# An encoder layer in one core: the down projection as seven half-depth products for eight, with its weights' sums kept in DRAM

## The chip, the cores and the metric

The kernel runs on one core of one Trainium2 chip. Its time is the device time of one execution in microseconds; before the change it is 1742.5 us, the median of three runs (1742.41 to 1742.98).

The engines of the core: TensorE (PE; PEld is its weight load) multiplies matrices into PSUM, which has eight banks of 2 KB per partition; VectorE (DVE), ScalarE (ACT) and GpSimd (POOL) work elementwise; SyncE (SP) issues DMAs, as ACT and GpSimd may too. Each engine takes its own instructions strictly in order, and a waiting instruction holds everything behind it.

## The reference

One layer on two sequences of 1024 and 256 tokens, T = 1280 in all, in float32: a wide input projection, neighbourhood attention and a gated short convolution, their merge, an output projection and a LayerNorm, and then the part that the change touches:

```python
h = dwconv3(x @ ffn_w_up + ffn_b_up, ffn_conv_w, ffn_conv_b)      # 1024 -> 2 x 2816
h_gate, h_val = jnp.split(h, 2, axis=-1)
f = (jax.nn.gelu(h_gate) * h_val) @ ffn_w_down + ffn_b_down       # 2816 -> 1024
return layer_norm(DEEPNORM_ALPHA * x + f, ln2_g, ln2_b)
```

The gated h is 2816 wide, that is 22 k-tiles of 128; w_down is 2816 x 1024; the result has ten token tiles of 128 x 1024.

## The kernel before

Every matmul of float32 data is made in three passes of a shorter float type: an operand is split into a high part (ACT's cast) and a low part (DVE's subtraction), `split2`, and high x high, low x high and high x low are added in PSUM (`passes`, L57). The order of all engines is written out by hand (`tc.manual_schedule`): the order in which the Python code issues an instruction is the order on its engine. Tiles come from pools with a fixed number of buffers; an instruction that writes a buffer waits until the last user of the old contents is done.

The stages in order: V and the first splits (to 60 us); the input projection, 18 pairs of column tiles (60 to 503 us); attention, with the convolution branch's product beside it (to 830 us); the merge, the output projection, the first LayerNorm (to 900 us); the up projection, 22 pairs (to 1428 us); the down projection and the second LayerNorm (to the end).

Both wide projections already use a seven-product scheme (class `Sevens`): weights and activations are cut in quarters, sums of quarters are formed, and seven products of half size stand for eight. A product is a slot of 24 matmuls of 320 columns; `at_slot(n, f)` puts side work behind slot n's weights and evictions. In slot n, ACT and DVE prepare the weights of product n+2 (`weights`) and evict product n-1 (`evict`, L154). The input projection has 126 slots; the pairs of gates are in slots 70 to 125. V is written to `v_dram` by `v_out` and read back in parts of four head pairs (`v_load`, `v_split`); the first part is loaded in slot 112 (NS - 14) into a pool of its own (vfp).

The up projection ends in a convolution, a gelu on ACT, a product on GpSimd, and a store of each of the 22 tiles of h to `h_dram` (L958 to L960). The down projection (L1012 to L1242) is a plain product. It takes the ten token tiles in three groups of 4, 3 and 3; a group holds two PSUM banks for each tile (two halves of 512 columns) and runs over the 22 k-tiles:

```python
for n in range(n0, n0 + FFT - DEEP):
    for at, t in enumerate(ts):
        for half in range(2):
            dn_mm(banks[t, half], n, at, half, n == n0, False)
    dn_next()
```

`dn_next` loads and splits a k-tile of h and of w_down a few steps ahead (`dn_split`: `fh`/`fl`, `wd`); the first ten w_down tiles stay in SBUF for the later groups, the others are loaded and split again. The last five k-tiles of a group are taken token by token, and after each token comes the second LayerNorm (`token`): sum (L1147), `mean` (ACT squares and centres, GpSimd multiplies by the gain, L1158), `var` and `rstd`, `finish` on DVE for 768 columns (L1161) and `finish_pool` on GpSimd for the rest (L1165), and the store. DVE has one list for all of this: splits, residual sums, evictions and LayerNorm stand one behind another.

Of the kernel before, what the change touches and what calls it, by code (L numbers as in the profile page):

```python
# [39 lines left out]
def encoder_kernel(ctx: ExitStack, tc: tile.TileContext, a: dict, y_prompt, y_sample):  # L40
# [352 lines left out]
    def yc_load(j):  # L393
        ycf.append(up_tile("o"))
        nc.sync.dma_start(out=ycf[j], in_=yc_dram[j])
# [68 lines left out]

    C0, REST = slice(0, 512), slice(512, T)
    for n, f in ((NS - 14, lambda: v_load(0)), (NS - 6, lambda: (yc_load(0), yc_load(1))), (NS - 5, lambda: (yc_load(2), yc_load(3)))):
        pr7.at_slot(n, f)
# [46 lines left out]
    for j in range(2, NP):  # L514
        yc_split(j, REST)
    up.release()
# [10 lines left out]
    at.tile([P, NT, P], F32, tag="vf", name="vf")  # L527
# [139 lines left out]
    v_split(0, 0)  # L667
    head_load(1)
    for n in range(units + LAG_V):
# [4 lines left out]
        if n == 1:  # L674
            v_split(0, 1)
# [29 lines left out]
    vfp.release()  # L705
# [306 lines left out]
    GROUPS = (range(0, 4), range(4, 7), range(7, NT))  # L1012
    DEEP = 5
    RES, NRING, NH = 10, 6, DEEP + 3
    ND = len(GROUPS) * FFT
    hs, ws, loaded = {}, {}, {}

    def dn_load(n):
        if n >= ND:
            return  # L1020
        g, i = divmod(n, FFT)
        c0, cn = GROUPS[g][0] * P, len(GROUPS[g]) * P
        hr = dnraw[:, 2, n % 2 * 512:n % 2 * 512 + cn]
        nc.sync.dma_start(out=hr, in_=h_dram[i][:, c0:c0 + cn])
        wr = None
        if g == 0 or i >= RES:
            wr = dnraw[:, n % 2, :]
            nc.sync.dma_start(out=wr, in_=a["w_down"][i * P:(i + 1) * P, :])
        loaded[n] = hr, wr, cn

    def dn_split(n):
        if n >= ND:
            return
        i = n % FFT
        hr, wr, cn = loaded.pop(n)
# [35 lines left out]
    for n in range(NS + 3):  # L1071
# [21 lines left out]
        if n == NS - 5:  # L1093
            for m in range(2):
                dn_load(m)
        if n == NS - 3:
# [6 lines left out]
            dwb = pool("dwb")  # L1103
        run_slot(n)
        if NS - 3 <= n <= NS:
# [8 lines left out]
    ss, zs, ys = [], [], {}  # L1114
# [4 lines left out]
    def residual_rows(n):  # L1119

        if n == 1:
            bd.append(dy.tile([P, D], F32, tag="z", name="bd", bufs=3))
# [5 lines left out]
        if n == 11:  # L1128
# [228 lines left out]
```

## Time and profile before

| | |
|---|---|
| profiled execution | 1741.4 us, span 1739.6 us |
| median of three runs | 1742.5 us |
| TensorE busy | 1693.5 us (97%), 10080 matmuls |
| DVE, ACT, GpSimd busy | 67%, 39%, 26% |
| DMA | 203.5 MB, mean 117 GB/s |

A busy matmul is counted from its start to a modelled end, and the matmuls overlap; what one costs is the spacing of starts. Shares of a stage are read from the table by stretches, not from the page's totals. In that table "PEclk" is the granted TensorE clock (1.00 is 2.4 GHz), "DMA share" the mean busy share of 16 DMA engines.

### The profile page before, as it was taken

To read this page: it belongs to the slowest core of one execution; us is meant where nothing else is said; L and a number is where in the kernel's file an instruction comes from. 1 tells how busy PE (TensorE), PEld (TensorE's weight loads), DVE (VectorE), ACT (ScalarE), POOL (GpSimd) and SP (SyncE) were. 2 spreads that over 40 slices of the span, in tenths; PEclk is the share of its full clock that TensorE was granted. 3 is DMA by queue.
4 is the path that set the end of the run, shared out by engine and by line. 5 is a ranking of instruction groups with operands and counts; after the bars stand their busy time and mean duration, and the time that the engine had idled before them with its cause. 6 is when DMAs were issued, how large, how long until landed. Compare 5 with 4: busy or idle time off the path is not lost.

```text
span 1739.6 us, 25955 instructions
## 1 busy us (share of the span) xinstructions
PE 1693.5 (97%) x10080; PEld 1567.2 (90%) x10080; DVE 1168.3 (67%) x1828; ACT 671.2 (39%) x1068; POOL 454.3 (26%) x368
## 2 busy tenths in 40 slices
PE   9999999999999998999998999999999999999997
PEld 7999999999988886778798999999999998888886
DVE  8466567434467774754698888888888887545455
ACT  4423323333246774323453333333333344333332
POOL 1222122212226663500113323332333220030202
PEclk9999999999999997999999999999999999999999
DMA  6276121222285632332301212211222137516262
GB/s 221 85 230 196 58 80 49 99 97 105 74 319 182 197 108 92 137 135 82 136 14 66 69 63 67 79 68 59 72 79 68 52 121 234 212 57 224 89 213 89
DMA packets 68923, 203.53 MB, mean 117 GB/s; under 512 B 7360, under 2 KB 19904, under 8 KB 68800
## 3 DMA queue, kind: packets, MB, share of 16 engines
q1 hardware_dynamic: 63040, 177.75, 30.3%
q0 software_dynamic: 3456, 15.73, 2.6%
q10 hardware_dynamic: 2304, 8.39, 1.2%
q8 instruction: 80, 1.31, 0.3%
q14 instruction: 43, 0.35, 0.1%
HBM read 145.48 MB, written 56.36 MB: 116 GB/s over the span
## 4 chain that ended last, share of the span: by engine, by line
PE 86%; DVE 7%; issue 3%; ACT 3%; DMA 1%; POOL 0%; ACTq 0%; POOLq 0%; DVEq 0%; SPq 0%
PE ps_x L57 52%; PE ps_dn L57 17%; PE ps_o L57 3%; PE ps_v L57 3%; PE ps_ch L548 3%; PE ps_ch L57 2%; PE o_ps L57 2%; PE s_ps L57 1%; PE t_ps L605 1%; DVE ul L69 1%; DVE c L154 1%; DVE xl L69 1%; DVE ml L69 0%; PE pz L844 0%; DMA x_dram<-ya 0%
## 5 line engine op out<-in xcount | busy, mean ns | idle before, releaser
L57 PE MATMUL ps_x<-xh,ul 128*128 128x320 f32 x2240 | 695.1, 310 | 8.0 <-DVE ul L69 7.5
L57 PE MATMUL ps_x<-xh,uh 128*128 128x320 f32 x2240 | 693.0, 309 | 3.7 <-ACT uh L72 3.1
L57 PE MATMUL ps_x<-xl,uh 128*128 128x320 f32 x2240 | 693.1, 309 | 1.9 <-DVE xl L69 1.9
L57 PEld LDWEIGHTS ps_x<-xh,ul 128*128 128x128 f32 x2240 | 421.9, 188 | 13.7 <-DVE ul L69 13.7
L57 PEld LDWEIGHTS ps_x<-xh,uh 128*128 128x128 f32 x2240 | 421.9, 188 | 4.5 <-ACT uh L72 3.7
L57 PEld LDWEIGHTS ps_x<-xl,uh 128*128 128x128 f32 x2240 | 421.8, 188 | 3.0 <-DVE xl L69 3.0
L69 DVE TENSOR_TENSOR ul<-ur,uh 128x512 fp32r<-128x512 f32 x240 | 199.4, 832 | 207.3 <-ACT uh L72 207.0
L72 ACT CAST uh<-ur 128x512 fp32r<-128x512 f32 x240 | 147.5, 616 | 330.1 <-PE ps_x L57 287.4
L57 PE MATMUL ps_dn<-wd,fh 128*128 128x512 f32 x880 | 271.4, 389 | 1.3 <-DVE dnraw L154 1.3
L154 DVE TENSOR_TENSOR c<-ps_x,c 128x640 f32<-128x640 f32 x275 | 220.6, 813 | 0.4 <-PE ps_x L57 0.3
L57 PEld LDWEIGHTS ps_dn<-wd,fh 128*128 128x128 f32 x880 | 165.2, 188 | 36.3 <-issue 1.0
L129 POOL TENSOR_TENSOR ur<-ur 128x512 f32<-128x512 f32 x40 | 56.5, 1414 | 510.1 <-DVE ul L69 510.1
L57 PE MATMUL ps_dn<-wd,fl 128*128 128x512 f32 x440 | 171.2, 389 | 0.0
L69 DVE TENSOR_TENSOR ul<-us,uh 128x512 fp32r<-128x512 f32 x38 | 71.0, 1867 | 55.1 <-ACT uh L72 55.1
L57 PEld LDWEIGHTS ps_dn<-wd,fl 128*128 128x128 f32 x440 | 82.6, 188 | 17.0
L943 ACT ACTIVATE o<-c,vec 128x1280 f32<-128x1280 f32 x43 | 62.5, 1458 | 83.8 <-DVE c L154 83.8
L946 DVE SCALAR_TENSOR_TENSOR o<-c,vec,o 128x1023 f32<-128x1023 f32 x86 | 89.2, 1037 | 1.6 <-ACT o L943 1.6
L959 POOL TENSOR_TENSOR o<-o 128x1280 f32<-128x1280 f32 x22 | 65.4, 2974 | 93.5 <-ACT o L958 80.8
L1158 POOL TENSOR_TENSOR z<-z,g 128x1024 f32<-128x1024 f32 (+1 forms) x10 | 23.2, 2316 | 252.9 <-issue 158.8
L1048 DVE TENSOR_TENSOR wd<-dnraw,wd 128x1024 fp32r<-128x1024 f32 x46 | 56.1, 1220 | 36.6 <-ACT wd L1047 36.5
L947 DVE SCALAR_TENSOR_TENSOR o<-c,vec,o 128x1023 f32<-128x1023 f32 x86 | 77.9, 905 | 3.0
L592 POOL TENSOR_TENSOR sp<-sp,stat 128x384 f32<-128x384 f32 (+1 forms) x80 | 59.5, 746 | 72.5 <-DVE stat L591 52.3
(202 smaller groups left out, 2341.9 us busy)
## 6 DMA issues: line engine op xcount, KB each, us to landing
dnraw<-in_w_down SPq DMA_DIRECT2D x46, 512.0 KB, 4.0
ur<-in_w_up SPq DMA_DIRECT2D x44, 512.0 KB, 3.5
ur<-in_w_in SPq DMA_DIRECT2D x36, 512.0 KB, 3.6
qk_dram<-o SPq DMA_DIRECT2D x48, 320.0 KB, 4.6
h_dram<-o SPq DMA_DIRECT2D x22, 640.0 KB, 2.9
sg_dram<-c SPq DMA_DIRECT2D x16, 640.0 KB, 2.9
dnraw<-h_dram SPq DMA_DIRECT2D x44, 192.0 KB, 2.4
dnraw<-h_dram SPq DMA_DIRECT2D x22, 256.0 KB, 3.7
```

Source lines behind the costliest of these rows:

```text
L57: nc.tensor.matmul(out, lhsT=l, rhs=r, start=(first and i == 0), stop=(last and i == n - 1))
L69: nc.vector.tensor_tensor(dst, p, q, ALU.subtract)
L72: nc.scalar.copy(hi, src)
L129: nc.gpsimd.tensor_tensor(a22, a12, a11, ALU.subtract)
L154: nc.vector.tensor_tensor(d, ps, q, ALU.add)
L548: nc.tensor.matmul(ps[:, :cn], lhsT=l, rhs=r, start=(i == 0), stop=(i == len(ops) - 1))
L592: nc.gpsimd.tensor_tensor(sp[:, :nk], sp[:, :nk], st[:, 2:3].to_broadcast([P, nk]), ALU.mult)
L943: nc.scalar.activation(o, c, AF.Identity, bias=beff[:, f:f + 1], scale=cw[1][:, f:f + 1])
L946: nc.vector.scalar_tensor_tensor(o[:, s + 1:s + n], c[:, s:s + n - 1], w0, o[:, s + 1:s + n], ALU.mult, ALU.add)
L947: nc.vector.scalar_tensor_tensor(o[:, s:s + n - 1], c[:, s + 1:s + n], w2, o[:, s:s + n - 1], ALU.mult, ALU.add)
L959: nc.gpsimd.tensor_tensor(o, o, u, ALU.mult)
L1048: nc.vector.tensor_tensor(wt[:, 1], wr, wt[:, 0].bitcast(F32), ALU.subtract)
```

## The change

Seven products for eight now hold for the down projection too. h (22 k-tiles x 1280 tokens) is cut in quarters by k-tiles (0 to 10, 11 to 21) and by tokens (two halves of 640, five tiles each), w_down by k-tiles and by columns (two halves of 512). A product p has depth 11 k-tiles, five token tiles and 512 columns, so it holds five PSUM banks; the order is p = 1, 5, 6, 7, 4, 2, 3. "Step q" is k-tile q mod 11 of the product number q div 11.

- **Weights.** The seven quarter sums of w_down are formed and split under the input projection (`wd_load`, `wd_step`): 11 sets, each with two rows of w_down read, four DVE differences, seven splits, and seven stores of 512 KB into `wd_dram`. Three sets lie in slots 31 to 69, one of eleven steps per slot; eight lie in slots 72 to 115, two steps per slot. The stores leave from two buffers (pool wdp), which `v_out` now uses as well.
- **SBUF.** To make room, the pool "up" has three "o" tiles and two "wr" tiles for five "o"; the pool vfp is gone: V's parts have two buffers in the pool of attention, the first is loaded when that pool opens, and it is split at units 2 and 3 in place of before unit 0 and at unit 1.
- **The down projection.** Weights come from `wd_dram` by GpSimd's DMA queue, eight buffers, seven steps ahead (`dn_weights`). h comes by SP in half tiles (`dn_load`, eight buffers); for p = 5, 6, 7 and 2 a DVE sum or difference of 640 columns is formed in `dsum` or in place, and every product splits its own 11 operands (`dn_prep`), five steps ahead. The seven products are added into the ten row tiles `ys` by `dn_evict`, on top of the residual. The residual's rows are loaded and scaled beside the products (`beside`).
- **LayerNorm.** Tokens 5 to 9 are finished under p = 2, tokens 0 to 4 in the last product, whose last six k-tiles are taken token by token.

The bank of t-th token tile in product n is number (5n + t + 4) mod 8: tiles 3 and 4 of a product take the banks of tiles 0 and 1 of the one before.

The core of the diff:

```diff
+    def wd_step(i, step):
+        b11, b12, b21, b22 = quarters[i]
+        def keep(p, src):
+            wd = wd_tile()
+            split2(wd[:, 0].bitcast(F32R), wd[:, 1].bitcast(F32R), src)
+            nc.sync.dma_start(out=wd_dram[p, i], in_=wd)
+        (lambda: keep(1, b11), lambda: diff(b11, b12, b11), lambda: keep(2, b21), lambda: keep(5, b11), lambda: keep(3, b22),
+         lambda: diff(b12, b22, b12), lambda: diff(b11, b22, b11), lambda: keep(7, b12), lambda: keep(6, b11),
+         lambda: diff(b11, b21, b11), lambda: keep(4, b11))[step]()
+    for i in range(NH):
+        first = 28 + 14 * i + 3 if i < 3 else 72 + (i - 3) * 11 // 2
+        pr7.at_slot(first - (3 if i < 3 else 2), lambda i=i: wd_load(i))
+        for step in range(11):
+            pr7.at_slot(first + (step if i < 3 else step // 2), lambda i=i, step=step: wd_step(i, step))
...
-            staged["v", j] = (vfp if j % 2 == 0 else at).tile([P, NT, P], F32, tag="vf", name="vf")
+            staged["v", j] = at.tile([P, NT, P], F32, tag="vf", name="vf", bufs=2)
...
-    v_split(0, 0)
...
-        if n == 1:
-            v_split(0, 1)
+        if n in (2, 3):
+            v_split(0, n - 2)
...
-    GROUPS = (range(0, 4), range(4, 7), range(7, NT))
-    DEEP = 5
-    RES, NRING, NH = 10, 6, DEEP + 3
+    DORDER = (1, 5, 6, 7, 4, 2, 3)
+    PARTS_OF = {1: ((0, 0),), 5: ((0, 1), (1, 1)), 6: ((0, 0),), 7: ((0, 0), (0, 1)), 4: ((1, 1),), 2: ((1, 0),), 3: ()}
+    ND, LOOK, RAW, WLOOK, NRING = 7 * NH, 5, 3, 7, 8
...
+    def dn_prep(q):
+        p, k = DORDER[q // NH], q % NH
+        raws, s = hraws.pop(q), None if p == 1 else dsum[:, k, :]
+        if p == 5:
+            nc.vector.tensor_tensor(s, raws[0], raws[1], ALU.add)
+        if p == 6:
+            diff(s, s, raws[0])
+        if p == 7:
+            diff(raws[0], raws[0], raws[1])
+        hs[q] = dwa.tile([P, 2, HALF], F32R, tag="fd", name="fd", bufs=NRING)
+        split2(hs[q][:, 0], hs[q][:, 1], s if p in (5, 6, 3) else raws[0])
+        if p == 2:
+            diff(s, raws[0], s)
+        dn_load(q + RAW)
...
+    def dn_evict(p, t, ps):
+        (c11, c12), (c21, c22) = ((ys[u][:, L], ys[u][:, R]) for u in (t, t + HT))
+        if p == 1:
+            nc.scalar.copy(c12, ps)
+            add(c11, c11, ps)
+        if p == 5:
+            nc.scalar.copy(c22, ps)
...
+        if p in (2, 3):
+            add_sum(t, int(p == 3), ps)
...
+    def beside(p, k):
+        t, odd = divmod(k, 2)
+        if p == 1:
+            residual_rows(k)
+            if 4 <= k < 9:
+                nc.sync.dma_start(out=ys[k - 4][:, L], in_=x1_dram[k - 4][:, L])
+            if 5 <= k < 10:
+                residual(ys[k - 5][:, L], L)
...
+        if p == 2 and k > 0:
+            u = (k - 1) // 2 + HT
+            if odd:
+                zs[u] = z_tile("z")
+                mean(u)
+            else:
+                var(ss[u])
+                for _ in rstd(ss[u]):
+                    pass
+                finish(u, slice(0, CUT))
+                finish_pool(u, slice(CUT, D))
+                store(u, slice(0, D))
...
+    for n, p in enumerate(DORDER):
+        ps = [banks[(5 * n + t + 4) % 8] for t in range(HT)]
+        tail = DEEP if p == 3 else 0
+        for k in range(NH - tail):
+            q = n * NH + k
+            for t in range(HT):
+                dn_mm(ps[t], q, t, k == 0, k == NH - 1)
+            dn_next()
+            if p == 3 and k == 1:
+                dn_next()
+            dn_weights(q + WLOOK)
+            beside(p, k)
+        for t in range(HT):
+            if tail:
+                for k in range(NH - tail, NH):
+                    dn_mm(ps[t], n * NH + k, t, False, k == NH - 1)
+                token(t, ps[t])
+            else:
+                dn_evict(p, t, ps[t])
```

On DVE, two slots of the late input projection stood so before (`ul` is the low part of a slot's weights, `c<-ps_x` an eviction):

```order
L69 TENSOR_TENSOR ul<-ur,uh 128x512
L154 TENSOR_TENSOR c_4028<-ps_x_3997,c_4028 128x640
L69 TENSOR_TENSOR ul<-ur,uh 128x512
L154 TENSOR_TENSOR c_4028<-ps_x_4030,c_4028 128x640
L154 TENSOR_TENSOR c_3929<-ps_x_4030,c_3929 128x640
```

and stand so now (`wd` is a low part of a quarter sum, `o<-o` a difference of quarters):

```order
L69 TENSOR_TENSOR ul<-ur,uh 128x512
L154 TENSOR_TENSOR c_4334<-ps_x_4303,c_4334 128x640
L69 TENSOR_TENSOR wd<-o,wd 128x512
L69 TENSOR_TENSOR o<-o 128x512
L69 TENSOR_TENSOR ul<-ur,uh 128x512
L154 TENSOR_TENSOR c_4334<-ps_x_4341,c_4334 128x640
L154 TENSOR_TENSOR c_4213<-ps_x_4341,c_4213 128x640
```

Two operations of a set stand behind each slot's own, ahead of the next slot's weights.

On SP, at the start of the down projection, the loads and the last two stores of h stood so before:

```order
L960 DMA h_dram<-o_9142 128x1280
L1024 DMA dnraw<-h_dram 128x512
L1028 DMA dnraw<-in_w_down 128x1024
L1024 DMA dnraw<-h_dram 128x512
L1028 DMA dnraw<-in_w_down 128x1024
L960 DMA h_dram<-o 128x1280
L1024 DMA dnraw<-h_dram 128x512
```

and stand so now (`hr` is a half tile of h, `y` the residual's row tile):

```order
L994 DMA h_dram<-o 128x1280
L1059 DMA hr<-h_dram 128x640 x8
L994 DMA h_dram<-o 128x1280
L1059 DMA hr<-h_dram 128x640 x7
L1219 DMA y_14397<-x_dram 128x512
L1059 DMA hr<-h_dram 128x640 x2
L1219 DMA y_14398<-x_dram 128x512
```

The w_down loads have left SP; eight half tiles of h stand ahead of the last store of h, all others behind it, and half rows of the residual between them.

On DVE, one token's LayerNorm stood so before (L1147 is an eviction with its sum, L1161 the finish), with no split between a mean and the finish:

```order
L1184 RECIPROCAL lns<-lns 128x1
L1173 TENSOR_SCALAR lns<-lns 128x1
L1174 TENSOR_SCALAR lns<-lns 128x1
L1185 TENSOR_SCALAR lns<-lns 128x1
L1186 TENSOR_SCALAR lns<-lns 128x1
L1187 TENSOR_TENSOR lns<-lns 128x1
L1147 ISA y_14460,lns<-y_14460,ps_dn 128x512
L1147 ISA lns 128x1
L1179 TENSOR_SCALAR lns<-lns 128x1
L1161 SCALAR_TENSOR_TENSOR z<-z,lns,b_14002 128x768
```

and the last token of p = 2 stands so now (`fd<-dsum` is a split for p = 3, L1185 an eviction of p = 2):

```order
L1272 TENSOR_SCALAR ss_14416<-ss_14416 128x1
L1273 TENSOR_SCALAR ss_14416<-ss_14416 128x1
L69 TENSOR_TENSOR fd<-dsum,fd 128x640
L1278 TENSOR_SCALAR ss_14416<-ss_14416 128x1
L1283 RECIPROCAL ss_14416<-ss_14416 128x1
L1284 TENSOR_SCALAR ss_14416<-ss_14416 128x1
L1285 TENSOR_SCALAR ss_14416<-ss_14416 128x1
L1286 TENSOR_TENSOR ss_14416<-ss_14416 128x1
L1260 SCALAR_TENSOR_TENSOR z<-z,ss_14416,b_14396 128x768
L1185 ISA y_14397,ss_14407<-y_14397,ps_dn 128x512
```

The splits now stand within each token's LayerNorm, and the evictions of p = 2 behind the last finish of tokens 5 to 9.

## Rows read from the trace of the kernel before

**Rows 1.** The page: its head, and the shares of the chain.

```profile
span 1739.6 us, 25955 instructions
...
PE 1693.5 (97%) x10080; PEld 1567.2 (90%) x10080; DVE 1168.3 (67%) x1828; ACT 671.2 (39%) x1068; POOL 454.3 (26%) x368
...
PE 86%; DVE 7%; issue 3%; ACT 3%; DMA 1%; POOL 0%; ACTq 0%; POOLq 0%; DVEq 0%; SPq 0%
...
```

**Rows 2.** Busy time by stretch; its second line names the columns.

```profile
...
core 0: us, PE busy (x) PEld busy (x) DVE busy (x) ACT busy (x) POOL busy (x), PEclk, DMA share, GB/s
312.00:467.00 155.00, 155.00 (x1059) 155.00 (x1058) 64.31 (x90) 48.72 (x64) 33.39 (x26) 1.00 0.28 101
505.00:510.00 5.00, 4.55 (x12) 3.30 (x13) 3.45 (x6) 4.52 (x6) 0.00 (x0) 0.69 0.93 296
510.00:515.00 5.00, 3.87 (x18) 2.95 (x17) 3.35 (x9) 2.75 (x7) 0.91 (x2) 0.97 1.03 403
1445.00:1450.00 5.00, 5.00 (x24) 4.14 (x23) 5.00 (x4) 1.66 (x3) 1.82 (x1) 1.00 1.00 386
1450.00:1455.00 5.00, 5.00 (x24) 4.14 (x23) 1.50 (x3) 2.19 (x3) 0.00 (x0) 1.00 1.01 330
1480.00:1720.00 240.00, 240.00 (x1061) 198.72 (x1060) 121.27 (x195) 82.81 (x123) 23.81 (x14) 1.00 0.44 150
...
```

**Rows 3.** Groups of equal form, 1480 to 1720 us: busy us, mean ns | idle before.

```profile
...
L1048 DVE TENSOR_TENSOR wd<-dnraw,wd 128x1024 fp32r<-128x1024 f32 x32 | 39.1, 1221 | 29.4 <-ACT wd L1047 29.4
...
L1038 DVE TENSOR_TENSOR fl<-dnraw,fh 128x512 fp32r<-128x512 f32 x8 | 5.5, 685 | 0.5 <-ACT fh L1037 0.5
...
```

**Rows 4.** Timeline at the down projection's start: start us, us, engine, line, operation.

```profile
...
1428.86 0.47 PE L57 MATMUL ps_dn<-wd,fh 128*128 128x512 f32 x1 [0.80 <-DVE dnraw L154]
...
1443.86 2.96 POOL L959 TENSOR_TENSOR o<-o 128x1280 f32<-128x1280 f32 x1 [23.43 <-ACT o L958]
...
1446.85 0.32 SPq L960 DMA_DIRECT2D h_dram<-o  x1
...
```

**Rows 5.** Groups of equal form, 312 to 467 us.

```profile
...
L69 DVE TENSOR_TENSOR ul<-ur,uh 128x512 fp32r<-128x512 f32 x37 | 25.6, 693 | 75.4 <-ACT uh L72 75.3
L72 ACT CAST uh<-ur 128x512 fp32r<-128x512 f32 x37 | 23.0, 621 | 67.5 <-PE ps_x L57 66.8
...
```

**Rows 6.** DMA issues: engine, operation, count, KB each, median us to landing.

```profile
...
sg_dram<-c SPq DMA_DIRECT2D x16, 640.0 KB, 2.9
...
out<-z SPq DMA_DIRECT2D x8, 512.0 KB, 2.6
...
o<-yc_dram SPq DMA_DIRECT2D x4, 640.0 KB, 6.9
...
```

**Rows 7.** Timeline of the normalisation of two tokens, 1537 to 1550 us.

```profile
...
1537.51 0.21 DVE L1173 TENSOR_SCALAR lns<-lns 128x1 f32<-128x1 f32 x1
...
1540.13 1.01 DVE L1161 SCALAR_TENSOR_TENSOR z<-z,lns,b 128x768 f32<-128x768 f32 x1
...
1540.45 2.94 POOL L1158 TENSOR_TENSOR z<-z,g 128x1024 f32<-128x1024 f32 x1 [5.13 <-ACT z L1157]
...
1546.53 2.39 POOL L1158 TENSOR_TENSOR z<-z,g 128x1024 f32<-128x1024 f32 x1 [2.45 <-ACT z L1157]
...
1546.93 2.80 DVE L1161 SCALAR_TENSOR_TENSOR z<-z,lns,b 128x768 f32<-128x768 f32 x1
...
```

**Rows 8.** Timeline at the kernel's end.

```profile
...
1728.74 0.39 PE L57 MATMUL ps_dn<-wd,fh 128*128 128x512 f32 x1
...
1730.15 0.68 DVE L1150 TENSOR_TENSOR y<-y,ps_dn 128x512 f32<-128x512 f32 x1
...
```

**Rows 9.** Timeline of TensorE's matmuls after a stop, 505 to 510 us.

```profile
...
505.15 0.73 PE L548 MATMUL ps_ch<-yc,wh 128*128 128x512 f32 x2 [1.41 <-ACT wh L72]
...
507.50 1.05 PE L548 MATMUL ps_ch<-yc,wh 128*128 128x512 f32 x2
...
508.78 1.05 PE L548 MATMUL ps_ch<-yc,wh 128*128 128x512 f32 x2
...
```

More of the change, by code (lines that the diff above doesn't have):

```diff
@@ L463, in w_split, with wd_load @@
         split2(*wbr[d], raws[d])
+    NH = FFT // 2
+    wd_dram = dram.tile([8, NH, P, 2, 512], F32, name="wd_dram")
+    quarters = {}
+    def wd_load(i):
+        rows = [up_tile("o" if i > 3 and i % 2 == 0 else "wr") for r in range(2)]
+        for r, t in enumerate(rows):
+            nc.sync.dma_start(out=t[:, :D], in_=a["w_down"][(i + r * NH) * P:(i + r * NH + 1) * P, :])
+        quarters[i] = [t[:, c * 512:(c + 1) * 512] for t in rows for c in range(2)]
+    def wd_step(i, step):
[12 more added lines that the diff above has]
+            pr7.at_slot(first + (step if i < 3 else step // 2), lambda i=i, step=step: wd_step(i, step))
     C0, REST = slice(0, 512), slice(512, T)
-    for n, f in ((NS - 14, lambda: v_load(0)), (NS - 6, lambda: (yc_load(0), yc_load(1))), (NS - 5, lambda: (yc_load(2), yc_load(3)))):
+    for n, f in ((NS - 6, lambda: (yc_load(0), yc_load(1))), (NS - 5, lambda: (yc_load(2), yc_load(3)))):
         pr7.at_slot(n, f)
@@ L1102, in encoder_kernel @@
             dwa = pool("dwa")
-            dwb = pool("dwb")
+            for q in range(WLOOK):
+                dn_weights(q)
+            for q in range(RAW):
+                dn_load(q)
         run_slot(n)
-        if NS - 3 <= n <= NS:
+        if n == NS - 3:
+            dn_next()
+            dsum = dwa.tile([P, NH, HALF], F32, name="dsum")
+        elif NS - 3 < n <= NS:
+            dn_next()
+        if n == NS:
             dn_next()
@@ L1113, in encoder_kernel, with z_tile @@
     g2, b2 = (dy.tile([P, D], F32, name=n) for n in ("g2", "b2"))
-    ss, zs, ys = [], [], {}
+    ys = [dy.tile([P, D], F32, name=f"y{t}") for t in range(NT)]
+    ss = [dy.tile([P, 8], F32, name=f"ss{t}") for t in range(NT)]
+    zs, rest = {}, {}
+    L, R = slice(0, 512), slice(512, D)
+    def z_tile(name):
+        return dy.tile([P, D], F32, tag="z", name=name, bufs=5)
     def row_load(dst, n):
@@ L1127, in residual_rows @@
             nc.vector.scalar_tensor_tensor(br, br, ALPHA, bd[0], ALU.mult, ALU.add)
-        if n == 11:
+        if n == 10:
             row_load(g2, "ln2_g")
             row_load(b2, "ln2_b")
-    def y_load(t):
-        ys[t] = dy.tile([P, D], F32, tag="y", name="y2", bufs=4)
-        nc.sync.dma_start(out=ys[t], in_=x1_dram[t])
-    def y_residual(t):
-        nc.vector.tensor_tensor(ys[t], ys[t], gr, ALU.mult)
-        nc.vector.tensor_tensor(ys[t], ys[t], br, ALU.add)
-    def dn_mm(ps, n, at, half, first, last):
-        (fh, fl), wt, ts_, cs = hs[n], ws[n], slice(at * P, (at + 1) * P), slice(half * 512, (half + 1) * 512)
-        passes(ps, [(fh[:, ts_], wt[:, 0, cs]), (fl[:, ts_], wt[:, 0, cs]), (fh[:, ts_], wt[:, 1, cs])], first=first, last=last)
@@ L1189, in encoder_kernel, with token @@
     CUT = 768
-    def token(t, mm):
-        end = t == NT - 1
-        ss.append(lns_tile())
-        zs.append(dy.tile([P, D], F32, tag="z", name="z", bufs=3))
-        acc(t, 0, mm(0))
+    def token(t, ps):
+        end = t == HT - 1
+        zs[t] = z_tile("z")
         if t > 0:
@@ L1263, in encoder_kernel @@
     every.__exit__(None, None, None)
[L1264 removed]
+    for p in (dy, gp_b, dwa, const, dp):
         p.release()
```

150 lines of the change are left out of this document (70 added, 80 removed).

## The prediction

> **What bounds the kernel now.** I read the head of the page first, then the chain, then the table by stretches, then the timelines of the joints that the change touches. The head and the chain [rows 1]: TensorE is busy 97% of a span of 1739.6 us and holds 86% of the chain, so an edit pays only by matmuls taken away or by waits of TensorE. The page's DVE at 67% looks like room, but it is an average. The table by stretches [rows 2] shows the down projection running without a gap, 1061 matmuls in 240 us, 0.2262 us each, with DVE busy for 121 of the 240 and the DMA engines at 0.44. Matmuls overlap, so a row's own duration is no price; the spacing is. The late input projection (slots 72 to 115, 312 to 467 us) has TensorE at 100%, DVE at 64 of 155 us, DMA at 0.28.
>
> The sum is made against the profiled execution's own 1741.4 us; the median of the three runs, 1742.5, lies 1.1 above it, which I add at the end. A difference under 0.2% (3.5 us) is one that timing this kernel can't tell from none.
>
> **What goes.** Before: 22 k-tiles x 10 token tiles x 2 halves x 3 passes = 1320 matmuls. After: 7 products x 11 x 5 x 3 = 1155, in the same form. 165 x 0.2262 = **-37.3 us**, all on the path. The down projection starts at 1428.9 [rows 4] and ends with the last matmul at 1729.1 [rows 8], 300.2 us for 1320 x 0.2262 = 298.6: it lost 1.6 us to PSUM banks that it needed at once; the new one needs five banks in its first step, so **-1**. From here a step is 15 matmuls, 3.39 us, and a product 11 steps, 37.3 us.
>
> **What is added under the input projection.** Per quarter set of w_down 7 splits and 4 differences, 11 sets. A split is an ACT cast of 0.62 and a DVE subtraction of 0.69 [rows 5], then a store of 512 KB, which lands in 2.6 us when alone [rows 6]. Eight sets lie in slots 72 to 115: 88 DVE operations x 0.69 = 61 us on top of 64 [rows 2], 125 of 155; on ACT 56 x 0.62 = 35 on top of 49. Bytes: 8 x (1.05 read + 3.67 written) = 38 MB, 243 GB/s on top of 101; 344 against the 368 of a full queue (below). So neither engine nor queue is over its limit, but both are close. The store buffers are two: a cast waits until the store before last has landed. Two splits thus take 0.62 + 0.69 + 2.6 = 3.9 us, where 56 in 155 us allow 5.5. TensorE has its weights two slots (7 us) ahead. Nearest bounds: 0, and 15 if stores land in 5 us (a rival, below). I take **+3**.
>
> **Attention.** The first V load leaves slot 112 and stands after the pools change; V's split moves from ahead of the first scores to units 2 and 3. It now goes through a queue that is full from 505 to 515 us, at 0.93 and 1.03 [rows 2]: 0.66 MB, 2 us; the split it leaves was on the chain. Bounds -1 and +3; I take 0.
>
> **Joint A: first to second product.** PSUM has eight banks, a product holds five, so t=3 of each new product needs the bank of t=0 of the old one. That bank's eviction stands on DVE behind everything of the old product: five preparations ahead, and here the residual's five half rows. TensorE wants it at 1428.9 + 37.3 + 2.0 (t=0 to 2) = 1468.2. What DVE needs first is data. SP sends eight h loads, then the store of the last h tile, which waits for ACT's gelu and GpSimd's product (today the store is issued at 1446.85 [rows 4]; 1445.2 by my working, since five DVE splits of 640, 0.82 us estimated from the 0.69 at 512 and the 1.22 at 1024 [rows 3], replace three pairs of 1.9), and only then the other h loads. GpSimd's weight loads 7 and on stand behind the same product. From 1445.2 the queue must bring: the store 0.66, h for steps 8 to 16 (3 x 0.33 + 6 x 0.66), five half rows 1.31, some 1.2 left of three broadcast rows, and weights 7 to 18, which are issued meanwhile, 6.3 MB: 14.4 MB in all. Three full stretches moved 403, 386 and 330 GB/s [rows 2]; their sum over that of their shares is 368. 14.4 / 0.368 = 39.1, to 1484.3, then a residual (2 x 0.68), a preparation (1.62) and the add (0.68): 1488.0, 20 us late. At 403 GB/s it is 16, at 330 it is 24; if the queue served h ahead of weights, 8.1 MB / 0.368, it is 3. I take **+18**, nearer to the shared queue, as no row shows one queue preferred.
>
> The Trainium skill ("DMA: Bandwidth & Descriptors", section "Anatomy of one DMA") puts the moving part of a transfer at bytes / 436 GB/s. By that figure the 14.4 MB would take 33 us and joint A would cost about 13; none of these stretches reached it, and the measured rate stands in the sum.
>
> At the second joint (p=5 to 6) 13.6 MB come in 37.3 us, again just the queue's rate: **+1** (0 to 6). The later joints have 10.7 to 12.7 MB: 0.
>
> **Joint B: sixth to seventh product.** In p=2 DVE also normalises tokens 5 to 9, and these stand in line with the preparations and ahead of p=2's evictions. After a mean, ACT squares and centres, and GpSimd's multiply starts 2.9 us later and takes 2.4 [rows 7]. While GpSimd multiplies, a DVE operation on SBUF waits: the 768-column finish takes 1.01 us free and 2.80 beside it [rows 7]. One token with its two preparations: multiply over at 5.35, subtraction and difference 1.6, variance, root and reciprocal 1.25 (six small operations of 0.21), finish 1.0 = 9.2, wait for GpSimd's add of 256 columns 0.9 (estimate: a quarter of 2.4, and its start), two more operations 1.6 = 11.7 us, or 10.2 where p=3 is prepared (no difference), against two steps, 6.8 us. From the end of p=4: 1.1 + 3.2 of preparation, 2 x 11.7, 2 x 10.2, a last 8.4, and the eviction 0.7 = 57.2; TensorE wants the bank at 37.3 + 2.0. That is 18 late. Without DVE's waits for GpSimd the pairs take 9.25 and 7.6, the last 6.6: 45.4, 6 late. I take **+16**, near the end that the 2.80 speaks for.
>
> Of these waits the Trainium skill ("SBUF — State Buffer", section "SBUF: two separate sides") says that a GpSimd operation and a DVE one with two SBUF inputs lock each other out for a whole instruction. By it joint B costs 18, without it 6; rows 7 bear the lock out.
>
> **Clock and tail.** After 1.4 us without a matmul, 505 to 510 us ran at a granted 0.69 of 2.4 GHz, partly at the lower level of 1.2, its matmuls 0.43 us apart for 0.23 [rows 2, 9]; some 2.2 us lost. Two long stops: **+4** (0 to 5). At the end a token has 18 matmuls, 4.1 us, for GpSimd's 2.4 + 0.9 and a DVE that waits for it; the last eviction comes 1 us after TensorE today [rows 8], I expect 2: **+1** (0 to 3).
>
> Sum: -38.3 + 3 + 18 + 1 + 16 + 4 + 1 = +4.7; 1741.4 + 4.7 + 1.1 = **1747 us**.
>
> **Rivals.** *The joints hold.* If h is served first (A 3 to 10) and GpSimd's multiplies fall beside DVE's waits for ACT (B 6 to 10), the stops are short, the clock stays, and the loss is 8 + 8 + 2 + 4 = 22: 1741.4 - 38.3 + 22 + 1.1 = 1726, faster. For it: TensorE never waited in this stage, though the same LayerNorm ran there. Against: then each token had 6.8 us of its own. It decides at a total loss of 35. *The store buffers bind under the projection.* One mechanism: splits wait for stores that share the queue with w_down's loads. At a landing of x the 56 splits take (1.31 + x) / 2 each; the point is x = 4.2. At 5 they take 177 us, 22 over, less 7 of lead: 15 instead of 3, 1759, slower. For it: 344 of 368 GB/s; loads of 640 KB took 6.9 us in a full queue [rows 6]. Against: stores of 640 KB land in 2.9 in this very stage [rows 6].
>
> **How the numbers follow.** Both joints as worked out: 0.52, own range 1737 to 1757; within it 0.08 faster, 0.17 same, 0.27 slower. Joints hold: 0.28 (0.27 faster, 0.01 same). Store buffers bind: 0.16, slower; the remaining 0.04 half and half. Faster 0.37, same 0.18, slower 0.45. Low end 1718 (A 4, B 6, no clock loss, 4 for the rest), high end 1762 (A 22, B 18, clock 5, projection 11, 2 for the rest).
>
> **What would show it.** In the new profile: 1155 ps_dn matmuls 0.226 apart; TensorE's longest waits at the second and the seventh product, both on DVE evictions; DMA share near 1.0 from 1445 to 1485 us; DVE subtractions of up to 3 us beside GpSimd's multiplies in p=2; stores of wd landing in under 4 us; TensorE full up to 467 us. Wrong would be a gap-free down projection (then about 1705), or waits of TensorE before 467 us.

## The result, and the profile after

The changed kernel takes 1786.19 us (1783.19 to 1786.67) where the one before takes 1742.57 beside it: a ratio of 1.0246, interval 1.0229 to 1.0264. It is slower, and 39 us above the forecast of 1747, outside the range. The profiled execution takes 1786.1, its span is 1784.3.

The head of the page after, to be held against [rows 1]: TensorE has lost share, and HBM is written 97 MB.

```profile
span 1784.3 us, 26243 instructions
PE 1683.1 (94%) x9907; PEld 1555.3 (87%) x9915; DVE 1288.8 (72%) x2003; ACT 690.7 (39%) x1120; POOL 495.4 (28%) x445
HBM read 187.68 MB, written 96.73 MB: 159 GB/s over the span
```

Where the 44.7 us of span went is read from the first and last matmul of each stage:

| stretch | before | after | difference | forecast |
|---|---|---|---|---|
| to the first score matmul of attention | 503.1 | 533.1 | +30.0 | +3 |
| attention, to the first matmul of the output projection | 232.4 | 234.7 | +2.3 | 0 |
| output projection and LayerNorm | 124.2 | 124.1 | -0.1 | 0 |
| up projection, first to last matmul | 568.1 | 569.9 | +1.8 | 0 |
| to the first ps_dn matmul | 1.1 | 5.2 | +4.1 | 0 |
| down projection, first to last matmul | 299.8 | 305.5 | +5.7 | +0.7 |
| to the end | 10.9 | 11.7 | +0.8 | +1 |

The stages are cut at these matmuls, so their borders differ from the rounded ones of the section on the kernel before: there the output projection begins at 735.5 us and the up projection at 859.7. The -1 of the forecast stands in the down projection's row.

So most of it is lost before the down projection begins. The waits of TensorE (engine, tile, line; what it waited for; us in total, times, longest) after, in the whole span:

```profile
PE ps_dn L57 <- DVE y L1179: 14.2, 1, 14.2
PE ps_dn L57 <- DVE ss L1185: 14.2, 1, 14.2
PE ps_x L57 <- DVE ul L69: 14.0, 17, 2.8
PE ps_x L57 <- ACT uh L72: 13.2, 7, 3.6
PE ps_dn L57 <- DVE dnraw L154: 4.9, 1, 4.9
PE ps_dn L57 <- ACT fd L72: 4.4, 1, 4.4
```

The first two are joints A and B, each one single stop on a DVE eviction (L1179 adds the first product, L1185 the sixth). The next two belong to both wide projections; the same question for 312 to 533 us alone, the end of the input projection, gives 17.3 us in 16 stops, where before had none:

```profile
PE ps_x L57 <- ACT uh L72: 9.9, 5, 3.6
PE ps_x L57 <- DVE ul L69: 7.4, 11, 1.0
```

These answer for 17.3 of the 30.0. In the other 12.7 TensorE counts as busy, but makes fewer matmuls. The table by stretches (columns as in [rows 2]) shows the stage, and then the time round one stop of 3.1 us at 385.5:

```profile
312.00:467.00 155.00, 143.59 (x918) 139.99 (x917) 106.14 (x147) 65.82 (x100) 28.13 (x21) 0.96 0.79 286
380.00:385.00 5.00, 4.89 (x34) 4.63 (x33) 3.33 (x4) 0.62 (x1) 0.84 (x1) 1.00 0.94 270
385.00:390.00 5.00, 1.38 (x6) 0.72 (x4) 1.86 (x3) 1.18 (x3) 0.00 (x0) 0.87 0.74 301
390.00:395.00 5.00, 4.82 (x18) 4.82 (x19) 4.87 (x7) 2.47 (x4) 1.29 (x1) 0.50 0.60 243
395.00:400.00 5.00, 5.00 (x34) 5.00 (x33) 3.23 (x5) 2.83 (x4) 0.00 (x0) 0.94 0.70 276
```

From 390 to 395 TensorE is busy 4.82 of 5 us and makes 18 matmuls for the usual 34: a granted 0.50, the lower of its two levels. Before, the first of these stretches was full at 1.00 [rows 2]. Not every stop has such a stretch behind it. In this stage there are four; just ahead of them TensorE stood for 1.5, 3.1, 3.4 and 4.6 us:

```profile
344.40:347.80 3.40, 3.40 (x15) 3.40 (x14) 2.62 (x4) 1.28 (x3) 0.49 (x1) 0.50 0.56 224
388.70:395.50 6.80, 6.10 (x22) 5.71 (x23) 6.13 (x9) 3.01 (x4) 1.29 (x1) 0.50 0.59 236
436.50:439.90 3.40, 3.38 (x13) 3.38 (x14) 3.32 (x5) 1.14 (x2) 1.29 (x2) 0.50 0.54 112
484.30:487.70 3.40, 3.35 (x12) 3.35 (x13) 2.19 (x4) 2.64 (x4) 0.00 (x0) 0.50 0.39 151
```

They hold 62 matmuls in 16.2 busy us, which at the spacing of before (155 us for 1059, [rows 2]) would take 9.1: some 7 of the 12.7 us are the lower clock. The other 5 or 6 lie round the stops themselves, at full clock.

Why the stop? ScalarE in that stretch (start, us; what ended the idle time in brackets):

```profile
381.47 0.62 ACT L72 CAST wd<-wr 128x512 fp32r<-128x512 f32 x1 [3.68 <-DVE wr L69]
387.46 0.62 ACT L72 CAST wd<-o 128x512 fp32r<-128x512 f32 x1 [5.37 <-DMA wd_dram<-wd]
387.98 0.61 ACT L72 CAST uh<-ur 128x512 fp32r<-128x512 f32 x1
```

The cast of a quarter sum waits 5.37 us until a store has left its buffer, and the cast of the projection's next weights (uh) stands behind it. Over 312 to 533 us ScalarE waited so 24 times:

```profile
ACT wd L72 <- DMA wd_dram<-wd: 54.8, 24, 6.4
```

The page's list of DMA issues (KB each, median us to landing) makes a store look quick:

```profile
wd_dram<-wd SPq DMA_DIRECT2D x77, 512.0 KB, 3.3
```

For 376 to 392 us alone it is 5.3; the next set's two rows (o) and two loads of ur are in the queue with the stores:

```profile
wd_dram<-wd SPq DMA_DIRECT2D x4, 512.0 KB, 5.3
ur<-in_w_in SPq DMA_DIRECT2D x2, 512.0 KB, 5.1
o<-in_w_down SPq DMA_DIRECT2D x2, 512.0 KB, 7.7
```

The down projection's two stops in the table by stretches: the queue is full ahead of the first, as forecast, and not at the second (the forecast's 1445 to 1485 us lies 38 later here).

```profile
1480.00:1500.00 20.00, 20.00 (x90) 16.57 (x89) 8.80 (x8) 4.46 (x7) 7.82 (x11) 1.00 1.00 345
1500.00:1520.00 20.00, 10.84 (x37) 7.68 (x35) 7.92 (x11) 1.66 (x3) 1.52 (x3) 0.79 1.07 393
1520.00:1540.00 20.00, 10.45 (x33) 8.35 (x34) 15.76 (x21) 6.03 (x11) 1.06 (x2) 0.61 0.79 268
1720.00:1740.00 20.00, 5.79 (x15) 4.31 (x14) 15.74 (x31) 7.63 (x13) 8.47 (x9) 0.58 0.56 169
```

At joint A VectorE waits for two residual rows (y, from the first product's list), and the five adds that free the banks (L1179) come behind all five rows. Between the last such wait and the adds lie 15.0 us in which it waits for no landing: four rounds of residual, sum and split. SyncE's issue of the last store of h, then VectorE:

```profile
1483.41 0.32 SPq L994 DMA_DIRECT2D h_dram<-o  x1
...
1507.70 0.69 DVE L1175 TENSOR_TENSOR y<-y,dnraw 128x512 f32<-128x512 f32 x1 [9.63 <-DMA y<-x_dram]
1513.77 0.69 DVE L1175 TENSOR_TENSOR y<-y,dnraw 128x512 f32<-128x512 f32 x1 [2.22 <-DMA y<-x_dram]
...
1528.81 3.08 DVE L1179 TENSOR_TENSOR y<-y,ps_dn 128x512 f32<-128x512 f32 x5
```

### The profile page after: what moved, and what is told of

The parts are those of the page before. It is cut to its first block, busy times and chain, and to the rows that moved or that the text cites. A ratio compares the mean times of both kernels' runs of the same rounds, so it can differ in the third digit from the quotient of the medians.

```text
span 1784.3 us, 26243 instructions
## 1 busy us (share of the span) xinstructions
PE 1683.1 (94%) x9907; PEld 1555.3 (87%) x9915; DVE 1288.8 (72%) x2003; ACT 690.7 (39%) x1120; POOL 495.4 (28%) x445
## 5 line engine op out<-in xcount | busy, mean ns | idle before, releaser
L57 PE MATMUL ps_x<-xh,uh 128*128 128x320 f32 x2240 | 698.6, 312 | 13.7 <-ACT uh L72 13.2
L57 PEld LDWEIGHTS ps_x<-xh,uh 128*128 128x128 f32 x2240 | 426.6, 190 | 15.9 <-ACT uh L72 15.1
L57 PE MATMUL ps_dn<-wd,fd 128*128 128x512 f32 x1155 | 272.7, 399 | 38.2 <-DVE y L1179 14.2
L57 PEld LDWEIGHTS ps_dn<-wd,fd 128*128 128x128 f32 x1155 | 222.8, 193 | 87.9 <-DVE y L1179 14.9
L1064 POOL DMA_DIRECT2D wd<-wd_dram x77 | 41.6, 543 | 181.7 <-PE ps_dn L57 178.5
L127 POOL TENSOR_TENSOR ur<-us,ur 128x512 f32<-128x512 f32 x38 | 49.6, 1305 | 96.5 <-DVE ul L69 96.4
L112 POOL TENSOR_TENSOR us<-ur 128x512 f32<-128x512 f32 x38 | 50.1, 1319 | 94.5 <-DVE ul L69 47.3
L992 ACT ACTIVATE o<-o 128x1280 f32<-128x1280 f32 x22 | 28.0, 1273 | 119.9 <-DVE o L987 119.9
```

Of the source, the lines that this page charges most:

```text
L57: nc.tensor.matmul(out, lhsT=l, rhs=r, start=(first and i == 0), stop=(last and i == n - 1))
L112: nc.gpsimd.tensor_tensor(self.sums[i], a21, a22, ALU.add)
L127: nc.gpsimd.tensor_tensor(a11, self.sums[i], a11, ALU.subtract)
```

## Experiments

### What of the added work holds the input projection?

Theory 1 is the store buffers, theory 2 the added operations themselves, theory 3 the bytes. (The operations added are 121 of VectorE and 77 of ScalarE; an expectation below counts 143.) In the first three kernels the down projection reads tiles of w_down in place of the kept sums. **no_sums** takes all of the added work out:

```diff
-        pr7.at_slot(first - (3 if i < 3 else 2), lambda i=i: wd_load(i))
-        for step in range(11):
-            pr7.at_slot(first + (step if i < 3 else step // 2), lambda i=i, step=step: wd_step(i, step))
```

> The changed kernel without any work on w_down under the input projection: no loads, differences, splits or stores there; the down projection reads tiles of w_down of the same size and shape in place of the kept sums (its values are left out). The changed kernel reaches the first score matmul of attention at 533.1 us, the one before at 503.1. All theories of the input projection: 503 to 504 us here, and a whole time of 1786 - 30 = 1756 us. If the down projection (first to last ps_dn matmul, 305.9 us) changes by more than 2 us, what is kept in DRAM and where it lies matters there too.

**no_stores** keeps loads, differences and splits:

```diff
             split2(wd[:, 0].bitcast(F32R), wd[:, 1].bitcast(F32R), src)
-            nc.sync.dma_start(out=wd_dram[p, i], in_=wd)
```

> The changed kernel with the loads, differences and splits of w_down's sums but without their stores; the down projection reads tiles of w_down instead. Theory 1 (the two store buffers: ScalarE's cast of a sum waits until the store before last has landed, and the next weights' cast stands behind it): first score matmul at 503 to 506 us, no wait of ScalarE for a store, whole time about 1758. Theory 2 (the 143 added operations themselves fill VectorE and ScalarE, slowed beside GpSimd): at 518 us or later, whole time 1771 or more. Theory 3 (bytes: the full queue delays the loads of the projection's own weights): 503 to 506, like theory 1; the next kernel separates them.

**stores_only** keeps loads and stores, and leaves out differences (a second edit) and splits:

```diff
-            wd = wd_tile()
-            split2(wd[:, 0].bitcast(F32R), wd[:, 1].bitcast(F32R), src)
+            wd = quarters["rows", i][p % 2][:, :D].rearrange("p (b c) -> p b c", b=2)
             nc.sync.dma_start(out=wd_dram[p, i], in_=wd)
```

> The changed kernel with the same loads and the same 77 stores of 512 KB at the same places, but straight from the loaded rows: no difference and no split, so no operation of ScalarE or VectorE is added (the sums are left out). Theory 3 (bytes alone): TensorE still waits for its weights, first score matmul at 515 us or later. Theory 1 (a cast waiting for a store buffer): 503 to 506 us, whole time about 1757, although the same bytes move. Theory 2: 503 to 506 as well.

**third_buffer** leaves the dense sets and gives them a third buffer in an idle row tile:

```diff
+            wd = late[2][:, :D].rearrange("p (b c) -> p b c", b=2) if turn[0] % 3 == 2 else wd_tile()
```

> The changed kernel with its dense sets (two steps per slot, loads two slots ahead), and a third store buffer from the fifth set on. Theory 1 (two buffers, and landings of 5 to 8 us where a set's first stores share the queue with the next set's loads): a third buffer carries 1.31 + x up to 8 us without holding ScalarE more than one slot; the first score matmul comes at 508 to 518 us for 533.1, ScalarE's waits for stores fall from 54.8 us to under 25. Rival (the queue's mean rate, 344 of 368 GB/s, is the limit, and buffers only move the wait): 525 or later.

| kernel | first score matmul | TensorE's waits, 312 us to it | ScalarE for a store | time |
|---|---|---|---|---|
| after | 533.1 | 17.3 | 54.8 | 1786.2 |
| no_sums | 503.3 | 0 | - | 1756.0 |
| no_stores | 503.0 | 0 | 0 | 1753.1 |
| stores_only | 503.4 | 0 | - | 1755.1 |
| third_buffer | 512.2 | 5.5 | 20.7 | 1765.0 |

Neither the operations nor the bytes cost TensorE anything alone; only both together do, where a split must wait for a landing. stores_only moves more bytes a second than the changed kernel's 286 GB/s, and TensorE is full:

```profile
312.00:467.00 155.00, 155.00 (x1060) 155.00 (x1059) 64.35 (x90) 48.95 (x64) 33.16 (x26) 1.00 0.91 340
```

So the queue's rate is not the limit. With a third buffer 21 of the 30 us come back. That decides for theory 1. The down projection keeps its 305 to 308 us in all four, so its losses are its own.

**spread** thins the sets out:

```diff
-        first = 28 + 14 * i + 3 if i < 3 else 72 + (i - 3) * 11 // 2
+        first, n = (5 + 13 * i, 11) if i < 5 else (72 + (i - 5) * 23 // 3, 7)
```

> The changed kernel with the eleven sets spread more evenly: five (not three) sets at one step per slot from slot 5, six (not eight) in slots 72 to 116, eleven steps in seven slots. The same work in total. Theory 1: 42 stores instead of 56 in the late stretch, 3.7 us apart for 2.75; a store lands in 3.4 and two buffers carry that, so the first score matmul comes at 506 to 512 us, whole time 1759 to 1765. Theory 2: VectorE still has 66 x 0.8 = 53 us on top of 64 of 155, little better, 520 to 525 us. Theory 3: 29 MB for 38 in the late stretch, 508 to 515 us.

508.2 us to the first score matmul and 1760.8 in all: 25 of the 30 us back with the same work. **ring** adds the third buffer and loads four slots ahead.

> The kernel with spread sets (first score matmul at 508.2 us; ScalarE still waited 26.7 us for stores and 29.1 for loads of w_down between 312 and 520 us), with a third store buffer in the late sets and w_down's rows loaded four slots ahead for two. If buffers and landings are all that is left, 503 to 505.5 us, TensorE's waits on ul down to the 2.8 that every run has at the up projection and under 1.5 in this stage; whole time 1756 to 1758.5 for 1760.8. If it is the order on VectorE and ScalarE itself, 508 stays.

It gave 507.6 and 1757.5; the expected 503 to 505.5 was missed. Three kernels below have spread's input stage unchanged and reach attention at 504.6, 504.8 and 506.1, so a few us of this stage vary from one execution to another, and by time ring is not told from spread. The traces tell where the loss lies. In spread TensorE still waits three times, 0.7 us, after 312 us; in ring it does not wait there at all and keeps the full clock. The whole loss of ring lies before 312 us, where the early sets now begin at slot 5 and still have two buffers: TensorE makes 1690 matmuls there for the changed kernel's 1720, with four stops. Ring's stretches, and what it waits for from 60 to 312:

```profile
60.00:312.00 252.00, 249.26 (x1690) 247.44 (x1689) 200.14 (x249) 101.52 (x150) 56.42 (x40) 1.00 0.61 206
312.00:507.60 195.60, 195.60 (x1337) 195.60 (x1336) 142.27 (x186) 85.88 (x127) 44.55 (x36) 1.00 0.72 263
PE ps_x L57 <- DVE ul L69: 2.7, 4, 1.2
```

So the late sets are cured by buffers and earlier loads, and neither branch of the expectation is right as it stands.

### The start and the two joints of the down projection

Each of these is spread with one edit. **h_store**:

```diff
-        nc.sync.dma_start(out=h_dram[i], in_=o)
+        (nc.gpsimd if i > FFT - 3 else nc.sync).dma_start(out=h_dram[i], in_=o)
```

> The spread kernel with the stores of the last two tiles of h issued by GpSimd (right behind its product) in place of SyncE, so that no load of h stands behind a waiting store. Theory Q (SyncE's order): the first h loads go out 4 us earlier and the wait of TensorE at the down projection's first matmul falls from 5.0 to under 2; the loads of steps 8 and on no longer wait from 1459 to 1483 us, and the wait at the second product (14.7 + 4.9 behind it) falls by 6 or more. Theory F (the full queue, as predicted: 14.4 MB at 368 GB/s have to land first): the start wait 3 or more, the wait at the second product 12 or more. Whole time 1748 to 1753 by Q, 1757 or more by F.

1746.3 us, under both theories' times. The wait before the first ps_dn matmul (5.0 in spread) is gone: in spread SyncE issues the last store but one at 1428.7 and only behind it the first loads of h, 6.9 us before the last matmul of the up projection; here they leave 17.6 us before it. The wait of 4.9 at the second product (it stands just ahead of the long one, not behind, as the expectation has it) is gone as well, but the long one is 14.0 for 14.7:

```profile
PE ps_dn L57 <- DVE y L1179: 14.0, 1, 14.0
PE ps_dn L57 <- DMA wd<-wd_dram: 1.3, 1, 1.3
```

That looks as if the order on SyncE had nothing to do with joint A. But the length of a stop is the distance between two moments, and here both came earlier. Counted from the last matmul of the up projection (1435.96 in spread, 1433.27 here), the adds that free the banks begin after 67.3 us in spread and after 54.6 here, 12.7 earlier:

```profile
1503.23 3.08 DVE L1179 TENSOR_TENSOR y<-y,ps_dn 128x512 f32<-128x512 f32 x5
1487.85 3.08 DVE L1179 TENSOR_TENSOR y<-y,ps_dn 128x512 f32<-128x512 f32 x5
```

TensorE, without the stops of 5.0 and 4.9, is at the joint earlier by nearly as much. So the order on SyncE made both the start and the eviction late, and 14.0 us of joint A have another cause. The Trainium skill ("DMA: Bandwidth & Descriptors", section "Issuing engines are not separate DMA queues") says that another issuing engine saves only issue time, as all share the 16 DMA engines. The rate agrees: from 1460 to 1480 us the queue moves 380 GB/s in spread and 399 here. The 12.7 us came from loads that no longer stand behind a waiting store on one engine's list, which the section does not speak of.

**no_residual**:

```diff
-            if 4 <= k < 9:
-                nc.sync.dma_start(out=ys[k - 4][:, L], in_=x1_dram[k - 4][:, L])
-            if 5 <= k < 10:
-                residual(ys[k - 5][:, L], L)
```

> The spread kernel without the loads and the scaling of the residual's left half rows (five of 256 KB) under the first product; their add takes another operand (that part of the output is left out). Theory F (the queue's volume): 13.1 MB for 14.4, and 6.9 us less on VectorE: the wait at the second product falls from 14.7 to 8 to 12. Theory Y (VectorE's list is held by these rows themselves, whose loads stand behind all others and landed 18 us after their issue, VectorE idle 9.6 and 2.2 us for them): the wait falls to 0 to 5 and the fd wait of 4.9 behind it stays; whole time 1743 to 1750.

1747.8 us, in theory Y's range; the wait at the second product is 11.2, in theory F's 8 to 12, not theory Y's 0 to 5. The fd wait of 4.9, which theory Y would keep, is gone. Neither theory is borne out whole, and the edit cannot part them: it takes 1.31 MB out of the queue and ten operations (6.9 us) off VectorE, and the two stops together fall from 19.6 us to 11.2, by more than the 3.6 that 1.31 MB take at 368 GB/s.

**ln_late** gives each LayerNorm token two free steps between its mean and the rest, and takes two tokens out of the sixth product:

```diff
+        for u, begin, end in ((5, (2, 1), (2, 3)), (6, (2, 4), (2, 6)), (7, (2, 7), (2, 9)), (8, (3, 0), (3, 2)), (9, (3, 1), (3, 4))):
```

> The spread kernel with the LayerNorm of tokens 5 to 7 in three steps each under the sixth product (mean, two steps later the rest) and that of tokens 8 and 9 moved to the first five steps of the last product. Theory as predicted (GpSimd's 2.4 us multiply holds VectorE, and ten LayerNorm parts stand ahead of the evictions): wait at the seventh product 0 to 2 us for 14.2, and the lower clock after it (0.58 in 20 us) goes too, 4 us; whole time 1741 to 1746 for 1760.8. Rival (VectorE is late in this product whatever stands in it): 8 us or more stay, 1755 or more.

The wait of 14.2 at the seventh product is gone; 1751.1 us lie between the two ranges. The down projection is 295.1 for 305.4, so 10.3 came back, not 14.2 + 4: two waits for weights, 4.0 us together, are new, and beside all waits the matmuls lose as much as in spread (9.4 us for 9.6). The edit moves two tokens out of the product and parts each mean from its finish at once, so it does not tell the one's share from the other's. Why VectorE was late in the changed kernel is seen beside GpSimd's multiply (VectorE and GpSimd at the first token):

```profile
1687.55 2.39 POOL L1257 TENSOR_TENSOR z<-z,g 128x1024 f32<-128x1024 f32 x1 [2.31 <-ACT z L1256]
1688.06 2.56 DVE L69 TENSOR_TENSOR fd<-hr,fd 128x640 fp32r<-128x640 f32 x1 [3.17 <-ACT fd L72]
1690.55 0.81 DVE L69 TENSOR_TENSOR dsum<-hr,dsum 128x640 f32<-128x640 f32 x1
```

The same subtraction takes 0.82 us free and 2.56 here (2.46 to 2.56 at all five tokens), ending 0.7 behind the multiply, as the lock of the Trainium skill ("SBUF — State Buffer", section "SBUF: two separate sides") has it.

### Together, and what joint A is

**combo** puts the edits of ring, h_store and ln_late together.

> All changes to the changed kernel that helped alone: sets spread over slots 5 to 116 with a third store buffer and earlier loads, the last two stores of h from GpSimd, the LayerNorm of tokens 5 to 9 spread into the last product. If the gains add (ring 1757.45; minus 14.5 by the stores of h, minus 9.7 by the LayerNorm): 1733, range 1729 to 1738, faster than before's 1741.7. What is left then: a wait of 14 us at the second product. If the queue gives the gains back (the second product waits longer because everything before it is earlier): 1740 or more.

1737.9 us (1735.2 to 1740.3), ratio to the kernel before 0.9975, interval 0.9964 to 0.9985: 0.25% faster than before, little more than the 0.2% that the prediction counts as none. It lies at the slow end of the range expected: the single gains (14.5 and 9.7) were taken from whole times and held 3.6 and 3.4 us of an input stage that only varied. What TensorE still waits for in the down projection:

```profile
PE ps_dn L57 <- DVE y L1182: 14.0, 1, 14.0
PE ps_dn L57 <- DMA wd<-wd_dram: 4.6, 2, 3.6
PE ps_dn L57 <- ACT y L1204: 1.0, 1, 1.0
PE ps_dn L57 <- ACT fd L72: 0.6, 1, 0.6
```

**combo_raw** loads the first product's weights unsplit:

```diff
+            if q < NH:
+                nc.gpsimd.dma_start(out=ws[q][:, 1], in_=a["w_down"][q * P:(q + 1) * P, :512])
...
+        if p == 1:
+            split2(ws[q][:, 0], ws[q][:, 1], ws[q][:, 1].bitcast(F32))
```

> The combination, and the first product's weights loaded as raw quarters of w_down (256 KB for 512 KB each, split by ScalarE and VectorE under the down projection itself, so 11 stores fewer under the input projection). Theory F (14.4 MB in a queue of 368 GB/s hold the second product's first bank): 2.9 MB less, so the wait there falls from 14 by 7 to 8, whole time 1724 to 1728. Theory V (VectorE's line): eleven more operations of 0.69 stand ahead of it, so the wait does not fall or grows, 1733 or more.

The wait fell from 14.0 to 13.5 only; 1738.5 us, as combo: theory V's side. It is no fair test of theory F, though. Seven of the eleven smaller loads go out at 1422.8, before the last store of h; only four, 1.05 MB less, are in the stretch that F speaks of, and the eleven subtractions stand in the same list as the eviction. A stop of 3.6 us at the start is new, and the input stage, with 11 stores fewer, is 3.5 us shorter. The stretch from 1440 and the one from 1460 us, of combo and then of combo_raw:

```profile
1440.00:1460.00 20.00, 18.99 (x85) 15.41 (x84) 13.68 (x19) 5.03 (x7) 7.83 (x10) 1.00 0.82 291
1460.00:1480.00 20.00, 14.43 (x64) 11.61 (x62) 8.84 (x12) 2.18 (x3) 2.12 (x4) 0.91 1.10 399
```

```profile
1440.00:1460.00 20.00, 20.00 (x90) 16.56 (x89) 13.75 (x20) 5.63 (x9) 7.31 (x10) 1.00 0.70 224
1460.00:1480.00 20.00, 15.18 (x67) 12.22 (x66) 13.79 (x19) 5.30 (x8) 2.87 (x5) 0.98 1.10 400
```

The first has 224 GB/s for 291, the second, ahead of the late eviction, stays at 400: the bytes left a stretch that had room.

**combo_lazy** scales each residual row right ahead of its own add, **combo_lazy_y** also loads the rows four steps earlier:

```diff
-            if 5 <= k < 10:
-                residual(ys[k - 5][:, L], L)
...
+            residual(c11, L)
             add(c11, c11, ps)
```

> The combination, with the scaling of each residual half row moved from the steps of the first product to right ahead of its own add, so that the first eviction no longer stands behind five rows; the same bytes, the same operations. Theory V (VectorE's order): of the five rounds of 3.8 us (two residual operations 1.4, preparation 2.4) and the waits of 2.3 us for rows, 5.6 us and the later rows' waits leave the path: the wait at the second product falls from 14.0 to 3 to 8, whole time 1727 to 1733 for 1737.9. Theory F (volume: nothing VectorE needs has landed earlier): 12 or more stays, 1736 or more.

> As combo_lazy, and the five half rows are asked for four steps earlier (behind steps 0 to 4 instead of 4 to 8), ahead of h for the second product. Theory V: rows are no longer waited for, the wait falls by up to 3 us more. Theory F: what the rows gain, h loses, since both share the queue; the same wait within 2 us as combo_lazy, or more if SyncE stops at a row whose buffer is not free yet.

1740.2 and 1739.9 us, so no gain: theory F's time. The stop, 10.9 and 11.9 us, is neither theory's, and 6.8 and 6.5 more stand at the third product, where combo has 1.0. What VectorE waited for from 1450 to 1490 us in combo, and to 1500 in combo_lazy:

```profile
DVE y L1178 <- DMA y<-x_dram: 12.7, 4, 5.5
```

```profile
DVE dsum L1075 <- DMA hr<-h_dram: 12.8, 4, 4.8
```

With the rows out of the way, VectorE waits as long for h. This order does not cure it: whichever of the two stands first on VectorE, it waits some 12.7 us for data in a queue that already moves 400 GB/s.

Counted from the last matmul of the up projection, in us, one execution each, the kernels compare so:

| kernel | first ps_dn matmul | fourth tile of the second product | last ps_dn matmul |
|---|---|---|---|
| after | 5.2 | 67.7 | 310.8 |
| spread | 5.3 | 68.0 | 310.6 |
| h_store | 0.2 | 55.3 | 297.4 |
| no_residual | 5.2 | 58.5 | 300.2 |
| ln_late | 5.3 | 68.3 | 300.5 |
| combo | 0.2 | 55.1 | 289.0 |
| combo_raw | 3.9 | 59.7 | 292.9 |
| combo_lazy | 0.1 | 52.0 | 292.9 |

At full speed the fourth tile would come at 39.5. The order on SyncE moves it by 12.7 us and the residual's rows, their bytes and their work together, by 9.5; what holds the rest, no run shows.

## Why the prediction was wrong

- **"I take +3" for the work under the input projection: this step failed.** It cost 30.0. The mechanism stood among the rivals ("the store buffers bind", 0.16, 1759), but its point and its price were wrong. The point, a landing of 4.2 us, was worked out from means over 155 us: 56 splits, evenly spaced. The median landing was 3.4, on the safe side of it, and 24 of 56 casts waited all the same, 54.8 us: a set's splits come in a burst, and in the stretch shown the next set's two row loads are in the queue with its stores. The price of 15 was delay minus lead; it left out what follows a stop, the lower clock (some 7 us) and the matmuls round the stops (5 or 6). "TensorE full up to 467 us" was wrong, "stores landing under 4 us" right by the median, and no proof of anything.
- **-37.3 by 165 fewer matmuls: right.** From 1467.1 to 1772.6 us are 305.5 us: 1154 x 0.2262 = 261.0, the waits 33.1 (14.2, 14.2, 4.4, 0.3), and 11.4 of slower matmuls.
- **-1 at the start: not seen.** The start itself, for which the sum had no term, came 4.1 us later (5.2 us behind the up projection for 1.1). The two new preparations stand on VectorE ahead of the evictions of the last up-projection products, and their h comes late behind a store; h_store removed it. The text looked at SyncE's order only for joint A.
- **Joint A, +18: right in size, 14.2 + 4.4 = 18.6, partly by luck.** The last store of h goes out 16.3 us after the first ps_dn matmul, as in the sum, and the eviction begins 45.4 us behind it for 42.1. But the sum gave 39.1 of these to landings and 3.0 to VectorE (a residual and a preparation); in the trace the last landing that VectorE waits for comes after 30.4, and the four rounds behind it take 15.0. The two errors nearly cancel. The order on SyncE, which the sum took as given, is worth 12.7 us of the eviction (h_store). How much of the rest is the volume of 14.4 MB stays open: no run takes bytes alone out of that stretch.
- **Second joint, +1: right (0.3).**
- **Joint B, +16: right, 14.2,** by the mechanism named: a token takes VectorE 11.0 and 9.5 us for the 11.7 and 10.2 of the sum, and at each a subtraction is held by GpSimd's multiply. ln_late removed the stop.
- **Clock, +4: too small, 11.4.** Two stops of 14 us and one of 4.4 were priced from a row after one of 1.4, and 1.7 us lie behind the stop at the start, which had no term.
- **Attention 0: +2.3, inside its bounds. Tail +1: +0.8.** The up projection's +1.8 had no term.

The down projection was thus forecast 5 us too short, the input projection 27. Without the latter the kernel lies at 1753 to 1756 (no_stores, no_sums), inside the likeliest case's own range.

## What to carry to other kernels

A buffer that waits for a landing is not priced by mean rates: write out the burst (which splits and loads fall in the same 10 us) and ask what stands behind the waiting instruction on its engine. Work that hides alone as operations and alone as bytes can still cost when a small ring ties them together; leaving out one half at a time shows that in two runs. Gains read from a stage's own boundaries nearly added up here (13.2 for h_store and 10.1 for ln_late, 21.6 together in combo, by the last column above); gains read from whole times carry the scatter of every other stage. And a stop's length is the distance between two moments: an edit that brings both forward leaves it as long, so count each from a fixed event.

## What the runs showed that was not expected

- From the end of a stop of 3.1 us the clock was at 0.50 for 6.8 us, and 16 stops of 17.3 us together cost 30: 0.7 us more for each us of waiting.
- In a shared queue a 512 KB load took 7.7 us and a store 5.3, where a store of 640 KB took 2.9 before [rows 6]. The queue's best stretches of 20 us were at 399 to 404 GB/s, above the 368 that the sum used.
